# The inversion of 16-wide diagonal blocks, moved from VectorE to GpSimd

## The chip, the cores and the metric

The kernel runs on one core of one Trainium2 chip. The metric is the device time of one execution in microseconds (us). A core has five engines that run side by side: TensorE (PE in the profile; its weight loads are PEld), VectorE (DVE), ScalarE (ACT), GpSimd (POOL) and SyncE (SP), which here only issues DMAs. Each works through its own queue in order and waits on semaphores for the others.

## The reference

Two layers of a backbone on 128 context tokens and 1024 latent tokens, width 1024. Layer 0 is attention, layer 1 is recurrent: a retention part and an RWKV-7 part, each with 8 heads of 64, each in both directions. A feed-forward block follows each layer. The part that the change touches is the RWKV-7 scan:

```python
def rwkv7_scan(r, w, k, v, a_vec, b_vec, s0):
    def step(S, inp):
        rt, wt, kt, vt, at, bt = inp
        sa = jnp.einsum('bhvk,bhk->bhv', S, at)
        S = S * wt[:, :, None, :] + sa[..., None] * bt[:, :, None, :] + vt[..., None] * kt[:, :, None, :]
        return S, jnp.einsum('bhvk,bhk->bhv', S, rt)
    ...
    S, ys = lax.scan(step, s0, xs)
    return jnp.moveaxis(ys, 0, 1), S
```

## The kernel before

The kernel runs in stages: attention layer with its projections, feed-forward block, projections of the recurrent layer, the recurrence (`rec_scan`), its output projection, feed-forward block. The recurrence lies between about 2420 and 3000 us of the span.

`rec_scan` does not step token by token. The nine chunks of 128 tokens are taken for four heads at a time (two pairs of heads, both directions), which makes 18 units `m`. Within a unit the coupling of the tokens of a chunk is a triangular 128x128 matrix per head and direction, and its inverse is wanted. The loop over `m` builds unit `m` while it finishes earlier ones:

- `prep(m)` loads the unit's columns (F, V), and makes AR, BK, PC and HT on VectorE, ScalarE and GpSimd (lines 1149 to 1175).
- `amat(m, i)`, for i = 0 and 1, multiplies AR and BK on TensorE (line 1190) into two PSUM banks; VectorE writes the masked parts to TC, ARB and KK (lines 1192, 1193, 1194: one **mask group** for each of eight products). TC holds the triangular matrices.
- `inv16(m)` inverts the 16-wide diagonal blocks. ScalarE copies them out of TC (C, line 1225); they go to memory and come back with one block on each of 32 partitions (bts, BT: lines 1226, 1230); VectorE mirrors them for the other half (line 1231), which gives 64 partitions. MB starts as the unit matrix (line 1233, GpSimd). Then 15 steps, each of a product (line 1240, tf) and a sum (line 1241, MB), invert all blocks. Each instruction needs the one before it. Step j works on 15-j rows of j+1 columns, so an instruction has 15 to 64 elements on each of 64 partitions. VectorE **folds** the two halves (lines 1243 and 1244, into BT); the result goes out to memory and comes back spread over 128 partitions (mbs, ML: lines 1247, 1249), and is multiplied with a block mask into E (VectorE) and MM (GpSimd), line 1254.
- `values(m)` makes two products with KK (lines 1206, 1213).
- `levels(m-1)` widens the inverses of the unit before from 16 to 32, 64 and 128: for each level a masked copy (E, line 1270, GpSimd), transposes (1264), a masked product (WT, line 1272, VectorE), two matrix products (1275, 1280) with a ScalarE copy between (X, 1277), and merges on VectorE (1282, 1284). At the end VectorE writes Nf and Nb (line 1290).
- `chain(m-2)` carries the state through the unit (lines 1306 to 1340; Zs on GpSimd in line 1328).

BT, MB, C, ML and TC are few: one buffer each of BT, MB, C and ML, three of TC. In the first units, pieces of an output projection (lines 81 to 83, with VectorE's line 769) are woven in as filler. The order in which each engine's queue holds all this is fixed when the kernel is built: a scheduler runs through the program with a cost for every instruction, so a change of engine can reorder the queues of all engines in this stage.

Of the kernel before, what the change touches and what calls it, by code (L numbers as in the profile page):

```python
# [15 lines left out]
ALU = mybir.AluOpType  # L16
# [20 lines left out]
def dap(ap, offset, dims):  # L37
    return bass.AP(tensor=ap.tensor, offset=ap.offset + offset, ap=dims)
# [5 lines left out]
class Net:  # L44
# [1015 lines left out]
    def rec_scan(self, hp):  # L1060
        nc, I, O = self.nc, self.I, self.O
        hp.release()
        with ExitStack() as es:
# [155 lines left out]
            def inv16(m):  # L1219

                tc, bd, md = TC[m % NTC], bts[m % 2], mbs[m % 2]
                C = self.t(p1, [P, 4, 32], tag="C")
                for g in range(4):
                    gs = slice(32 * g, 32 * g + 32)
                    nc.scalar.copy(C[gs], tc[gs, :, gs])
                nc.sync.dma_start(bd.rearrange("u p i -> p u i"), C)
                bt = self.t(p1, [64, 256], tag="BT")
                for b in range(2):
                    src = dap(bd, b * 16 * 33, [[32 * 32, 16], [32, 16], [1, 16]])
                    nc.sync.dma_start(bt[16 * b : 16 * b + 16].rearrange("p (j i) -> p j i", i=16), src)  # L1230
                nc.vector.tensor_copy(bt[32:64], bt[0:32, ::-1])
                mb = self.t(p1, [64, 256], tag="MB")
                nc.gpsimd.tensor_copy(mb, eye)
                B3 = bt.rearrange("p (j i) -> p j i", i=16)
                M3 = mb.rearrange("p (i c) -> p i c", c=16)
                for j in range(15):
                    nr, ncl = 15 - j, j + 1
                    tt = self.t(p1, [64, 64], tag="tf")[:, : nr * ncl].rearrange("p (i c) -> p i c", c=ncl)
                    row, col = B3[:, j, j + 1 :].unsqueeze(2).to_broadcast([64, nr, ncl]), M3[:, j : j + 1, :ncl].to_broadcast([64, nr, ncl])
                    nc.vector.tensor_tensor(tt, row, col, op=ALU.mult)  # L1240
                    nc.vector.tensor_tensor(M3[:, j + 1 :, :ncl], M3[:, j + 1 :, :ncl], tt, op=ALU.add)  # L1241
                m2 = bt[0:32]
                nc.vector.tensor_copy(m2, mb[32:64, ::-1])
                nc.vector.tensor_tensor(m2, m2, mb[0:32], op=ALU.add)
                for b in range(2):
                    dst = dap(md, b * 256, [[512, 16], [16, 16], [1, 16]])
                    nc.sync.dma_start(dst, m2[16 * b : 16 * b + 16].rearrange("p (i c) -> p i c", c=16))
                ml = self.t(p1, [P, 4, 16], tag="ML")
                nc.sync.dma_start(ml, md.rearrange("u p c -> p u c"))
                sh = [P, 4, 8, 16]  # L1250
                bm = lambda i: blk[:, i, :].rearrange("p (b c) -> p b c", c=16).unsqueeze(1).to_broadcast(sh)
                MM, E = self.t(p, [P, 4, P], tag="MM"), self.t(p, [P, 4, P], tag="E")
                for t, i, eng in ((E, 1, nc.vector), (MM, 0, nc.gpsimd)):
                    eng.tensor_tensor(t.rearrange("p u (b c) -> p u b c", c=16), ml.unsqueeze(2).to_broadcast(sh), bm(i), op=ALU.mult)
                Q["MM", m] = MM, E
# [126 lines left out]
            for m in range(NH + 2):  # L1382
# [10 lines left out]
                for ops in ORDER:  # L1393
                    for o in ops:
                        if o == "c":
                            step(cha)
                        elif o == "l":
                            step(lev)
                        elif o == "f":
                            pull()  # L1400
                        elif o == "p" and m < NH:
                            prep(m)
                        elif m < NH and o == "a":
                            amat(m, 0)
                        elif m < NH and o == "b":
                            amat(m, 1)
                            if m == 0:
                                nc.scalar.dma_start(eye, I["k_eye"])
                                for t, n in ((blk, "k_blk"), (mE, "k_mE"), (mO, "k_mO"), (tri, "k_tri")):
                                    nc.scalar.dma_start(t, I[n].rearrange("l p c -> p l c"))  # L1410
                        elif m < NH and o == "i":
                            inv16(m)
                        elif m < NH and o == "v":
                            values(m)
# [637 lines left out]
```

## Time and profile before

| | |
|---|---|
| three runs | 3990.24, 3992.53, 3998.9 us (median 3992.53) |
| profiled execution, its own time | 3991.86 us |
| span of the profiled execution | 3990.1 us |
| busy over the span | PE 95%, PEld 89%, DVE 54%, ACT 31%, POOL 18% |
| mean granted clock of TensorE | 0.973 of full speed |

Busy is the time in which an engine executed an instruction. The profiled execution has marks for start and end of each instruction, and who released a wait is inferred from semaphores. Matmuls are pipelined and their ends are modelled, so TensorE's busy time is no exact measure of work. The instruction counts of the page are 5159 on DVE and 730 on POOL.

### The profile page before, as it was taken

To read this page: it belongs to the slowest core of one execution; us is meant where nothing else is said; L and a number is where in the kernel's file an instruction comes from. 1 tells how busy PE (TensorE), PEld (TensorE's weight loads), DVE (VectorE), ACT (ScalarE), POOL (GpSimd) and SP (SyncE) were. 2 spreads that over 40 slices of the span, in tenths; PEclk is the share of its full clock that TensorE was granted. 3 is DMA by queue.
4 is the path that set the end of the run, shared out by engine and by line. 5 is a ranking of instruction groups with operands and counts; after the bars stand their busy time and mean duration, and the time that the engine had idled before them with its cause. 6 is when DMAs were issued, how large, how long until landed. Compare 5 with 4: busy or idle time off the path is not lost.

```text
span 3990.1 us, 62872 instructions
## 1 busy us (share of the span) xinstructions
PE 3790.7 (95%) x23989; PEld 3559.6 (89%) x23989; DVE 2169.5 (54%) x5159; ACT 1250.4 (31%) x2930; POOL 711.9 (18%) x730
## 2 busy tenths in 40 slices
PE   8999997999999999998999998888888999999998
PEld 5899997999999999998989876776777999999998
DVE  5666665666454545345254656888875543343343
ACT  4555545555111111115232322233222411111112
POOL 3321202202100000012011232233322300000000
PEclk9999998999999999999999997999999999999999
DMA  6533316432222222213243434222223211111111
GB/s 203 150 105 91 95 52 163 126 85 88 67 80 64 85 64 80 69 46 116 87 129 102 163 123 142 66 70 63 64 64 103 64 38 45 41 37 43 43 40 53
DMA packets 378086, 339.98 MB, mean 85 GB/s; under 512 B 65428, under 2 KB 328720, under 8 KB 376248
## 3 DMA queue, kind: packets, MB, share of 16 engines
q1 hardware_dynamic: 359344, 324.37, 27.0%
q10 hardware_dynamic: 13160, 7.27, 0.7%
q0 software_dynamic: 5280, 4.31, 0.5%
q8 instruction: 190, 3.11, 0.3%
q14 instruction: 112, 0.92, 0.1%
HBM read 263.37 MB, written 72.38 MB: 84 GB/s over the span
## 4 chain that ended last, share of the span: by engine, by line
PE 78%; DVE 10%; DMA 5%; issue 3%; ACT 2%; POOL 1%; SPq 0%; ACTq 0%; DVEq 0%; POOLq 0%
PE mm L81 17%; PE mm L83 17%; PE mm L82 17%; PE o L522 3%; PE mm L390 2%; PE mm L392 2%; PE mm L391 2%; PE T L516 1%; DVE MB L1241 1%; DVE tf L1240 1%; PE mm L857 1%; PE A L1190 1%; PE mm L859 1%; PE mm L858 1%; PE S L558 1%
## 5 line engine op out<-in xcount | busy, mean ns | idle before, releaser
L81 PE MATMUL mm<-hH,wh 128*128 128x384 f32 x2544 | 865.1, 341 | 20.2 <-DVE nv L363 12.6
L82 PE MATMUL mm<-hL,wh 128*128 128x384 f32 x2544 | 860.6, 339 | 2.5 <-DVE hL L366 2.5
L83 PE MATMUL mm<-hH,wl 128*128 128x384 f32 x2544 | 859.8, 339 | 0.0
L769 DVE SCALAR_TENSOR_TENSOR x<-mm,mod,x 128x384 f32<-128x384 f32 (+2 forms) x896 | 431.5, 512 | 197.5 <-PE mm L83 195.8
L81 PEld LDWEIGHTS mm<-hH,wh 128*128 128x128 f32 x2544 | 480.0, 189 | 31.4 <-ACT wh L73 18.8
L82 PEld LDWEIGHTS mm<-hL,wh 128*128 128x128 f32 x2544 | 480.1, 189 | 5.6 <-DVE hL L366 2.7
L83 PEld LDWEIGHTS mm<-hH,wl 128*128 128x128 f32 x2544 | 480.0, 189 | 4.0 <-issue 2.9
L1692 POOL TENSOR_TENSOR gl<-fs,gh 128x384 fp32r<-128x384 f32 x132 | 140.4, 1063 | 1484.1 <-ACT gh L1691 1484.1
L74 DVE TENSOR_TENSOR wl<-wraw,wh 128x512 fp32r<-128x512 f32 (+2 forms) x360 | 217.9, 618 | 336.0 <-ACT wh L73 306.4
L82 PE MATMUL mm<-gl,owh 128*128 128x384 f32 x1056 | 353.0, 334 | 0.0
L83 PE MATMUL mm<-gh,owl 128*128 128x384 f32 x1056 | 352.9, 334 | 0.0
L81 PE MATMUL mm<-gh,owh 128*128 128x384 f32 x1056 | 350.4, 335 | 0.0
L1690 DVE TENSOR_TENSOR fs<-fs,mm 128x384 f32<-128x384 f32 x132 | 73.0, 553 | 430.3 <-PE mm L83 424.7
L73 ACT CAST wh<-wraw 128x512 fp32r<-128x512 f32 (+2 forms) x360 | 188.2, 530 | 205.5 <-DMA wraw<-in_w_ffn_in_dram 77.3
L73 ACT CAST owh<-owraw 128x1024 fp32r<-128x1024 f32 x60 | 62.9, 1049 | 489.7 <-PE mm L82 446.0
L390 PE MATMUL mm<-wh,hH 128*128 128x384 f32 x576 | 199.3, 346 | 3.8 <-ACT ist L408 3.7
L82 PEld LDWEIGHTS mm<-gl,owh 128*128 128x128 f32 x1056 | 198.3, 188 | 0.1
L83 PEld LDWEIGHTS mm<-gh,owl 128*128 128x128 f32 x1056 | 198.2, 188 | 0.0
L81 PEld LDWEIGHTS mm<-gh,owh 128*128 128x128 f32 x1056 | 197.8, 188 | 0.3 <-DVE x L769 0.3
L391 PE MATMUL mm<-wl,hH 128*128 128x384 f32 x576 | 195.3, 339 | 0.0
L392 PE MATMUL mm<-wh,hL 128*128 128x384 f32 x576 | 194.0, 338 | 0.0
L1689 ACT ACTIVATE fs<-mm 128x384 f32<-128x384 f32 x132 | 64.9, 492 | 383.5 <-PE mm L83 383.4
(385 smaller groups left out, 7437.8 us busy)
## 6 DMA issues: line engine op xcount, KB each, us to landing
wraw<-in_w_ffn_in_dram SPq DMA_DIRECT2D x352, 128.0 KB
aw<-in_w_ada_dram SPq DMA_DIRECT2D x160, 256.0 KB
owraw<-in_w_ffn_out_dram SPq DMA_DIRECT2D x44, 512.0 KB
F<-stg SPq DMA_DIRECT2D x34, 640.0 KB
stg<-st SPq DMA_DIRECT2D x12, 1536.0 KB
qkv<-ist SPq DMA_DIRECT2D x72, 192.0 KB
wraw<-in_w_in_attn_dram SPq DMA_DIRECT2D x64, 192.0 KB
nab<-rpbd SPq DMA_DIRECT2D x64, 192.0 KB
```

The lines of the kernel that those rows point to most:

```text
L73: nc.scalar.copy(hi, src)
L74: nc.vector.tensor_tensor(lo, src, hi, op=ALU.subtract)
L81: mm(out, lhsT=wh, rhs=xh, start=first, stop=False)
L82: mm(out, lhsT=wh, rhs=xl, start=False, stop=False)
L83: mm(out, lhsT=wl, rhs=xh, start=False, stop=last)
L390: mm(pt[:, :ncol], lhsT=hH[k][:, c], rhs=WH[k], start=k == 0, stop=False)
L391: mm(pt[:, :ncol], lhsT=hH[k][:, c], rhs=WL[k], start=False, stop=False)
L392: mm(pt[:, :ncol], lhsT=hL[k][:, c], rhs=WH[k], start=False, stop=k == KT - 1)
L522: nc.tensor.matmul(o, lhsT=pT[:, i * P : (i + 1) * P], rhs=vs(b + i), start=b + i == 0, stop=b + i == nk - 1)
L769: self.nc.vector.scalar_tensor_tensor(x[f][:, c], pt[:, a:b], self.mod[l][jg][:, f, cd : cd + 1], x[f][:, c], op0=ALU.mult, op1=ALU.add)
L1690: nc.vector.tensor_tensor(s, s, pg[1][:, :GW], op=ALU.mult)
L1692: nc.gpsimd.tensor_tensor(gl[:, sl], s, gh[:, sl], op=ALU.subtract)
```

## The change

The product and the sum of the 15 steps are issued on GpSimd instead of VectorE. Nothing else in the program text changes; operands, sizes and buffers are the same.

```diff
                 for j in range(15):
                     nr, ncl = 15 - j, j + 1
                     tt = self.t(p1, [64, 64], tag="tf")[:, : nr * ncl].rearrange("p (i c) -> p i c", c=ncl)
                     row, col = B3[:, j, j + 1 :].unsqueeze(2).to_broadcast([64, nr, ncl]), M3[:, j : j + 1, :ncl].to_broadcast([64, nr, ncl])
-                    nc.vector.tensor_tensor(tt, row, col, op=ALU.mult)
-                    nc.vector.tensor_tensor(M3[:, j + 1 :, :ncl], M3[:, j + 1 :, :ncl], tt, op=ALU.add)
+                    nc.gpsimd.tensor_tensor(tt, row, col, op=ALU.mult)
+                    nc.gpsimd.tensor_tensor(M3[:, j + 1 :, :ncl], M3[:, j + 1 :, :ncl], tt, op=ALU.add)
```

The queues change with it. VectorE, around the fold of one unit (BT_28734, MB_28738) in the steady part of the stage; TC_4880 belongs to the next unit. Before:

```order
L1241 TENSOR_TENSOR MB_28738<-MB_28738,tf_28782 64x15 [waits DVE_49]
L1284 COPY_PREDICATED MM_28464<-mO_24512,I_28809 128x512 [waits PE_49]
L1243 COPY BT_28734<-MB_28738 32x256 [waits DVE_49]
L1192 COPY_PREDICATED TC_4880_24532<-msk_4873_24523,A_29036 128x128 [waits PE_49]
L1193 COPY_PREDICATED ARB_4885_24537<-msk_4873_24523,A_29036 128x128
L1244 TENSOR_TENSOR BT_28734<-BT_28734,MB_28738 32x256 [waits DVE_49]
L1194 COPY_PREDICATED KK_4878_24528<-msk_4873_24523,A_29036 128x256
L1192 COPY_PREDICATED TC_4880_24532<-msk_4873_24523,A_29037 128x128 [waits PE_49]
```

In the changed kernel:

```order
L1284 COPY_PREDICATED MM_28464<-mO_24512,I_28676 128x512
L1243 COPY BT_28734<-MB_28738 32x256 [waits Pool_49]
L1192 COPY_PREDICATED TC_4880_24532<-msk_4872_24522,A_29024 128x128 [waits PE_49]
L1193 COPY_PREDICATED ARB_4884_24536<-msk_4872_24522,A_29024 128x128
L1194 COPY_PREDICATED KK_4877_24527<-msk_4872_24522,A_29024 128x256
L1244 TENSOR_TENSOR BT_28734<-BT_28734,MB_28738 32x256 [waits DVE_49]
L1192 COPY_PREDICATED TC_4880_24532<-msk_4872_24522,A_29025 128x128 [waits PE_49]
L1193 COPY_PREDICATED ARB_4884_24536<-msk_4872_24522,A_29025 128x128
L1194 COPY_PREDICATED KK_4877_24527<-msk_4872_24522,A_29025 128x256
L1272 TENSOR_TENSOR WT_28795<-I_28796,mE_24511 128x512 [waits PE_49]
L1192 COPY_PREDICATED TC_4880_24532<-msk_4873_24523,A_29036 128x128 [waits DVE_49,PE_49]
```

The fold's copy waits for GpSimd; the last four mask groups of the next unit (A_29024, A_29025, A_29036, A_29037) and a WT stand behind it, where before only two groups did.

GpSimd, from the unit matrix MB of that unit on. Before:

```order
L1233 COPY MB_28738<-eye_24521 64x256 [waits DVE_49]
L1167 TENSOR_TENSOR BK_5983_28910<-F_5978_28897,EN_28902 128x512 [waits DMAHW0_49,PE_49,Activation_49]
L1254 TENSOR_TENSOR MM_28464<-ML_28462,blk_24524 128x512 [waits DMAHW4_49]
L1270 TENSOR_TENSOR E_28602<-MM_28464,mE_24511 128x512 [waits Pool_49]
L1328 TENSOR_TENSOR Zs_28700<-SB_4888_24540,PC_27897 128x512 [waits PE_49]
L1165 TENSOR_TENSOR AR_5973_28880<-F_5969_28872,EL_28876 128x2x128 [waits PE_49]
L1270 TENSOR_TENSOR E_28660<-MM_28464,mE_24511 128x512 [waits DVE_49]
L1164 COPY PC_28871<-EL_28901 128x2 [waits Activation_49]
L1165 TENSOR_TENSOR AR_5982_28905<-F_5978_28897,EL_28901 128x2x128 [waits PE_49]
```

In the changed kernel:

```order
L1233 COPY MB_28738<-eye_24521 64x256 [waits DVE_49,Pool_49]
L1254 TENSOR_TENSOR MM_28464<-ML_28462,blk_24524 128x512 [waits DMAHW3_49]
L1270 TENSOR_TENSOR E_28602<-MM_28464,mE_24511 128x512 [waits PE_49,Pool_49]
L1240 TENSOR_TENSOR tf_28740<-BT_28734,MB_28738 64x15 [waits DMAHW6_49,DMAHW5_49,DVE_49]
L1241 TENSOR_TENSOR MB_28738<-MB_28738,tf_28740 64x15 [waits Pool_49]
L1167 TENSOR_TENSOR BK_5983_28910<-F_5978_28897,EN_28902 128x512 [waits DMAHW0_49,PE_49,Activation_49]
L1240 TENSOR_TENSOR tf_28743<-BT_28734,MB_28738 64x28 [waits Pool_49]
L1328 TENSOR_TENSOR Zs_28700<-SB_4888_24540,PC_27897 128x512 [waits PE_49]
L1241 TENSOR_TENSOR MB_28738<-MB_28738,tf_28743 64x14x2 [waits Pool_49]
L1240 TENSOR_TENSOR tf_28746<-BT_28734,MB_28738 64x39 [waits Pool_49]
```

The 30 instructions stand between the first E and the next unit's BK, with one BK, Zs, two AR, two PC and one E among them, and each waits for GpSimd itself. The two AR follow the sixth and the seventh pair. MM of the unit before goes ahead of the first.

SP, the transfers at the end of that unit's inversion. Before:

```order
L1247 DMA mbs_24563<-BT_28734 16x256 [waits DMAHW6_49]
L1226 DMA bts_24562<-C_29048 128x4x32 [waits DMAHW7_49,Activation_49]
L1249 DMA ML_28789<-mbs_24563 128x4x16 [waits DMAHW6_49,DMAHW5_49,DMAHW0_49]
L1230 DMA BT_29054<-bts_24562 16x16x16 [waits DMAHW7_49,DMAHW1_49]
L1230 DMA BT_29054<-bts_24562 16x16x16 [waits DMAHW2_49]
```

In the changed kernel:

```order
L1247 DMA mbs_24563<-BT_28734 16x256 [waits DMAHW6_49]
L1249 DMA ML_28789<-mbs_24563 128x4x16 [waits DMAHW7_49,DMAHW6_49,DMAHW5_49]
L1226 DMA bts_24562<-C_29048 128x4x32 [waits DMAHW0_49,Activation_49]
L1230 DMA BT_29054<-bts_24562 16x16x16 [waits DMAHW1_49,DMAHW0_49,Pool_49]
L1230 DMA BT_29054<-bts_24562 16x16x16 [waits DMAHW2_49]
```

The load of ML goes ahead of the store of the next unit's blocks.

## Rows read from the trace of the kernel before

**Rows 1.** The page, part 1: busy us, share of the span and instructions of each engine

```profile
PE 3790.7 (95%) x23989; PEld 3559.6 (89%) x23989; DVE 2169.5 (54%) x5159; ACT 1250.4 (31%) x2930; POOL 711.9 (18%) x730
```

**Rows 2.** Chain of waits of the recurrence stage: shares by line; start us, us, what

```profile
by line: DVE MB L1241 7.3%; DVE tf L1240 7.3%; issue 6.5%; PE A L1190 5.5%; DVE MM L1284 4.4%; DVE KK L1194 4.3%; PE I L1275 3.5%; PE I L1280 3.1%; PE mm L81 2.8%; DVE ARB L1193 2.7%; DVE TC L1192 2.7%; PE I L1264 2.7%; DVE WT L1272 2.6%; P
...
2553.88 1.20 DVE tf L1240
...
2823.68 1.14 DVE tf L1240
...
2853.02 1.14 DVE tf L1240
...
2942.74 1.14 DVE tf L1240
```

**Rows 3.** Windows: stretch, length, busy PE, PEld, DVE, ACT, POOL, clock, DMA share, GB/s

```profile
2500.00:2530.00 30.00, 29.66 (x250) 26.15 (x249) 28.06 (x81) 9.75 (x20) 7.45 (x7) 1.00 0.22 60
2820.90:2850.30 29.40, 25.88 (x219) 20.98 (x218) 25.45 (x74) 9.29 (x23) 10.20 (x12) 1.00 0.26 69
```

**Rows 4.** VectorE in order of time, one turn: start us, us, instruction, [idle before]

```profile
2839.59 0.29 DVE L1192 COPY_PREDICATED TC<-msk,A 128x128 f32<-128x128 int32 x1
...
2840.32 0.28 DVE L1192 COPY_PREDICATED TC<-msk,A 128x128 f32<-128x128 int32 x1
...
2841.15 0.67 DVE L1272 TENSOR_TENSOR WT<-I,mE 128x512 f32<-128x512 f32 x1
...
2843.12 0.72 DVE L1240 TENSOR_TENSOR tf<-BT,MB 64x15 f32<-64x15 f32 x1
...
2845.31 0.28 DVE L1243 COPY BT<-MB 32x256 f32<-32x256 f32 x1
...
2846.03 0.41 DVE L1244 TENSOR_TENSOR BT<-BT,MB 32x256 f32<-32x256 f32 x1
...
2846.69 0.28 DVE L1192 COPY_PREDICATED TC<-msk,A 128x128 f32<-128x128 int32 x1
...
2850.79 0.86 DVE L1254 TENSOR_TENSOR E<-ML,blk 128x512 f32<-128x512 f32 x1 [2.10 <-DMA ML<-mbs]
```

**Rows 5.** Line 1240, whole span: duration ns min/median/max

```profile
L1240 DVE TENSOR_TENSOR tf<-BT,MB x270: 158/201/1265, 2435.6 to 2956.9; 64x15 f32<-64x15 f32 x18, 64x39 f32<-64x39 f32 x18, 64x55 f32<-64x55 f32 x18, 64x63 f32<-64x63 f32 x18
```

**Rows 6.** GpSimd in order of time, two pieces of the stage

```profile
2669.86 1.76 POOL L1254 TENSOR_TENSOR MM<-ML,blk 128x512 f32<-128x512 f32 x1 [0.64 <-DMA ML<-mbs]
2671.70 1.27 POOL L1270 TENSOR_TENSOR E<-MM,mE 128x512 f32<-128x512 f32 x1
...
2833.18 0.19 POOL L1164 COPY PC<-EL 128x2 f32<-128x2 f32 x1
...
2842.52 1.29 POOL L1167 TENSOR_TENSOR BK<-F,EN 128x512 f32<-128x512 f32 x1 [5.52 <-ACT X L1277]
```

**Rows 7.** GpSimd by line, whole span: count, busy us, mean ns, idle before

```profile
L1270 POOL TENSOR_TENSOR E<-MM,mE 128x512 f32<-128x512 f32 x36 | 47.9, 1332 | 50.6 <-DVE MM L1284 27.8 <-DVE MB L1241 9.2 <-DVE tf L1240 6.5
L1167 POOL TENSOR_TENSOR BK<-F,EN 128x512 f32<-128x512 f32 x36 | 46.5, 1292 | 127.1 <-ACT BH L1170 50.3 <-ACT X L1277 37.8 <-issue 21.7
...
L1165 POOL TENSOR_TENSOR AR<-F,EL 128x256 f32<-128x256 f32 x36 | 26.8, 745 | 32.7 <-PE c L1336 32.7
...
L1328 POOL TENSOR_TENSOR Zs<-SB,PC 128x512 f32<-128x512 f32 x14 | 14.7, 1051 | 0.9 <-PE c L1314 0.9
...
L1164 POOL COPY PC<-EL 128x2 f32<-128x2 f32 x36 | 9.6, 268 | 87.7 <-ACT EL L1157 87.6
```

**Rows 8.** Lines 1254 and 437, whole span: duration ns min/median/max, forms

```profile
L1254 DVE TENSOR_TENSOR E<-ML,blk x18: 691/693/1773, 2459.2 to 2963.2; 128x512 f32<-128x512 f32 x18
L1254 POOL TENSOR_TENSOR MM<-ML,blk x18: 1269/1764/1772, 2459.2 to 2963.2; 128x512 f32<-128x512 f32 x18
...
L437 POOL TENSOR_TENSOR rm<-rm,rm x40: 451/461/1486, 99.9 to 575.1; 128x128 f32<-128x128 f32 x32, 128x512 f32<-128x512 f32 x8
```

## The prediction

> **What bounds the kernel now.** I read the page first, then the chain of waits over the recurrence stage, then that stage in windows, and last one turn of it on each engine. On the whole span the change looks harmless: GpSimd is busy 18% and VectorE 54% [rows 1], and TensorE carries the kernel. But an average over stages says nothing about the one stage that is edited. The inversion runs only there, from 2435 to 2960 us. In the chain of waits of that stage its two lines are the first two entries, 7.3% each, ahead of every TensorE line [rows 2]. Its first instruction recurs at a steady beat: from 2553.88 to 2942.74 us lie 13 turns, 29.9 us each, and the turn that I take apart begins at 2823.68 and ends at 2853.02, so it lasts 29.34 us [rows 2].
>
> In that turn VectorE is busy 25.45 of 29.40 us, TensorE 25.88, GpSimd 10.20 [rows 3]. TensorE's ends are modelled, so its number is a ceiling; VectorE's is work in one queue, in order. That queue makes the turn: the inversion starts at 2823.68, its last result is folded at 2845.31, the last diagonal mask of the next unit's scores is written at 2846.69 (0.28 us), and 6.05 us after its end, at 2853.02, the next inversion starts [rows 2, 4]. In those 6.05 us the diagonal blocks are copied, go out to memory and come back. So the turn is one loop: inversion, masks behind it in the queue, a trip through memory, the next inversion. Whatever holds the inversion longer or shorter moves the turn by as much.
>
> **What goes from VectorE.** 30 instructions a turn, 540 in all. Undisturbed one takes 0.20 us (median), but up to 1.27 us [rows 5]: where GpSimd runs a two-input instruction, VectorE's small product waits for its end, as the one at 2843.12, which took 0.72 us beside a GpSimd product of 1.29 us that began at 2842.52 [rows 4, 6]. VectorE gets back 6.0 us a turn at the median, more with these waits. That is not the gain, for the loop does not vanish: VectorE's fold (line 1243) now waits for GpSimd's last step, and the last four mask groups of the next unit stand behind that fold. The moved queue still closes the loop; only its parts get other lengths.
>
> **The new turn, part by part.**
>
> (a) From GpSimd's last step to the last mask on VectorE: the fold's copy 0.28, a mask group 0.73 (2839.59 to 2840.32), the fold's sum 0.41, a group 0.73, the transposed factor's product 0.67, a group 0.73, the last mask 0.28 [rows 4]. Together 3.83 us. The first two groups' score products do not depend on GpSimd, and each later product needs only a bank that an earlier group has freed.
>
> (b) From that mask to the next start, 6.05 us as now [rows 2, 4]: the same copies and the same two transfers. On SP's queue the load of the folded inverses (ML) now goes ahead of the blocks' store instead of behind it; it is issued early enough that neither waits for the other. On GpSimd MM (1.76 us) and the first E (1.27 us) now stand between two inversions [rows 6]. They need ML, which lands about 4.4 us after the fold's sum (2846.03 plus 0.41, to 2850.79, where VectorE's product on ML starts after a wait of 2.10 us [rows 4]), so they are through about 9 us after the last step (0.28 + 0.73 + 0.41 + 4.4 + 1.76 + 1.27 = 8.9), ahead of the 9.9 us of (a) and (b): covered, by 1 us.
>
> (c) The 30 steps on GpSimd. No row has so small a two-input instruction on GpSimd. The nearest: 128x128 at 0.46 us median [rows 8] and 128x512 at 1.27 us [rows 6]. That is 2.1 ns an element and 0.19 us fixed, and a copy of 2 elements at 0.19 us undisturbed [rows 6] fits that fixed part. The 15 products touch 680 elements a partition, the 15 sums as many, 1360 in all: 30 x 0.19 + 1360 x 0.0021 = 8.6 us. Each step needs the one before it; E, which needs MM, starts 0.08 us after its end (2669.86 + 1.76 to 2671.70) [rows 6]. 30 x 0.08 = 2.4 us. Together 11.0 us, or 0.37 us a step. Broadcast operands cost nothing extra that shows: MM has two and reaches 1.27 us undisturbed [rows 8].
>
> (d) The other GpSimd work now woven between the steps: one BK 1.29, one Zs 1.05, two AR 0.75 each, two PC 0.27 each, one E 1.33 [rows 7], 5.7 us. These means hold the collisions with VectorE's two-input instructions.
>
> The new turn: 3.83 + 6.05 + 11.0 + 5.7 = 26.6 us, against 29.34: 2.8 us less. Over 13 turns, 36 us. **The other terms:** the first four turns (2435 to 2554 us) also carry an output projection and TensorE is busy 29.66 of 30 us in their midst [rows 3], so I count nothing there; if that cover of TensorE work is thinner than it looks, the same 2.8 us a turn would add some 10 us of gain. The last inversion has no next turn; nothing. The new wait on VectorE (line 1243) has masks, E, Nf and Nb behind it, and ScalarE's block copy and TensorE's value products wait for those masks; that is (a) and (b). Who else waits on GpSimd: AR, which feeds the next unit's score products, now stands behind six and seven pairs of steps. By my count it is ready about 9 us after the inversion starts, and the two levels of products, masks and merges that follow it on TensorE and VectorE end some 2 us before GpSimd's last step (an estimate from the durations of this turn). That is the next thing to be late.
>
> The profiled execution took 3991.86 us (median of the runs 3992.53, so 0.7 us below it). 3991.86 - 36 = **3956 us**.
>
> **A rule that speaks against it.** On the same line and shape (1254, 128x512) VectorE took 0.69 us and GpSimd 1.27 us undisturbed, 1.84 times [rows 8]. The Trainium skill, "GPSIMD Engine Reference", section "Engine selection", says to keep elementwise products and sums off GpSimd, which is about twice as slow on two inputs. Two times VectorE's 0.20 us make a step 0.40 us, the 30 with their gaps 14.4 us, the turn 30.0 us and the kernel some 8 us slower (an estimate by that page); the trace's large shape agrees with the page, and no row shows whether the factor holds where the fixed part rules.
>
> **Rivals.**
>
> *The factor holds for small steps too.* 0.20 x 1.84 = 0.37 us, with gaps 0.45 us a step, 13.4 us; the turn is 29.0 us, 0.3 us less: 4 us, about 3988 us, no change. For it: the ratio in [rows 8]. Against it: the fixed part of a GpSimd copy is 0.19 us, no more than a whole VectorE step. Chance 0.11.
>
> *GpSimd has a floor and the loop lengthens.* If a small two-input step costs as much as the smallest that the trace has, 0.46 us, it is 0.54 us with its gap: 16.2 us, turn 31.8 us, 2.4 us longer, 13 times 32 us: 4024 us. It decides from 0.46 us a step with gap (13.8 us for the 30), where the turn is back at 29.34. For it: no smaller product is in the trace, AR's collisions and TensorE's idling may add to the loop, and a wait on GpSimd stands in VectorE's queue with everything behind it. Against: 128, 256 and 512 elements (0.46, 0.75, 1.27 us) lie on one line with the copy's fixed part [rows 6 to 8]. Chance 0.19.
>
> *TensorE becomes the bound.* If its 25.88 us a turn are real work, the turn stops at 25.9 us: 3.4 x 13 = 45 us, 3947 us. It would show if the steps on GpSimd were cheaper than my sum. Chance 0.10.
>
> That the change does not do what it says is excluded: all 540 instructions stand on GpSimd in the order of the changed kernel.
>
> **How the numbers follow.** My forecast has 0.60. A step can be cheaper than I take it: without the gap the 30 steps are 8.6 us and the turn 24.2 us, 67 us less, 3925 us. That and TensorE's bound are the lower end. The dearer ends are the two first rivals; the range reaches up over "no change", to 3997 us, and leaves out the lengthened loop (0.19). A change of 0.2% is about 8 us, which is what a measurement of this kernel can tell from none. Faster: 0.60 + 0.10 = 0.70; within: 0.11; slower: 0.19.
>
> **What would show it.** In the changed profile lines 1240 and 1241 on GpSimd with a mean near 0.29 us and starts about 0.37 us apart; turns of 26 to 27 us; VectorE's busy time at 19 us a turn or less (25.45 [rows 3] less 30 x 0.20), GpSimd's near 19 (10.20 and 8.6); the chain of this stage on GpSimd's two lines, then on the fold, masks and the two transfers. I am wrong if a step is spaced 0.46 us or more, if GpSimd waits for AR's or E's inputs in the midst of the steps, or if MM rather than the blocks' load starts the next inversion.

## The result, and the profile after

The changed kernel took 3947.65 us (median of four runs, 3943.83 to 3961.69), the kernel before beside it 3991.39 us: a ratio of 0.9893, 95% interval 0.9866 to 0.992. It is 1.1% faster; 3956 us was forecast. The profiled execution took 3943.83 us, its span is 3942.0 us, 48.1 us shorter than the span before.

The page, part 1 (busy us, share of the span, instructions), answers to [rows 1]; beneath it the shares by line of the chain of waits of the stage, as in [rows 2]:

```profile
PE 3785.3 (96%) x23989; PEld 3557.3 (90%) x23989; DVE 2057.6 (52%) x4619; ACT 1246.1 (32%) x2930; POOL 852.0 (22%) x1270
```

```profile
by line: DMA F<-stg 7.1%; PE A L1190 6.1%; issue 5.8%; POOL tf L1240 5.3%; POOL MB L1241 5.1%; PE I L1280 4.6%; PE c L1314 4.5%; PE A L1206 4.0%; PE I L1275 3.6%; PE I L1264 3.5%; PE mm L81 3.4%; PE A L1213 3.4%; PE mm L82 3.2%; PE mm L83 3
```

The 540 instructions stand on GpSimd. The steps have gone from the head of the chain to its fourth and fifth place; ahead of them are now the transfer of F and TensorE's score products (line 1190), which the prediction did not have there. The two lines by themselves (duration ns min/median/max), which answer to [rows 5]:

```profile
L1240 POOL TENSOR_TENSOR tf<-BT,MB x270: 207/260/1196, 2426.6 to 2913.7; 64x15 f32<-64x15 f32 x18, 64x39 f32<-64x39 f32 x18, 64x55 f32<-64x55 f32 x18, 64x63 f32<-64x63 f32 x18
```

```profile
L1241 POOL TENSOR_TENSOR MB<-MB,tf x270: 211/278/516, 2427.9 to 2913.9; 64x15 f32<-64x15 f32 x18, 64x39 f32<-64x39 f32 x18, 64x55 f32<-64x55 f32 x18, 64x63 f32<-64x63 f32 x18
```

A product costs 0.26 us on GpSimd where it cost 0.20 us on VectorE: 1.3 times. Those are medians. On the mean, which holds the waits beside the other engine, the order is reversed, 276 ns for 297 (count | busy us, mean ns | idle before, of the kernel before and of the change):

```profile
L1240 DVE TENSOR_TENSOR tf<-BT,MB 64x15 f32<-64x15 f32 (+2 forms) x270 | 80.2, 297 | 5.8
L1240 POOL TENSOR_TENSOR tf<-BT,MB 64x15 f32<-64x15 f32 (+2 forms) x270 | 74.5, 276 | 51.0 <-DVE BT L1231 35.6
```

So the 30 instructions themselves hardly shorten the inversion: on the mean of thirteen steady turns their durations add up to 9.1 us before and 8.2 us now. What shortens it is the company that they keep: VectorE had some 33 other instructions between the first and the last of them, GpSimd has 7 (durations of 14.9 and 5.5 us in all). One inversion of each kernel as a window (stretch, length, busy PE, PEld, DVE, ACT, POOL, clock, DMA share, GB/s), in which VectorE ran 63 instructions before and GpSimd runs 38 now:

```profile
2823.68:2845.31 21.63, 18.82 (x155) 14.83 (x155) 20.68 (x63) 4.15 (x10) 6.64 (x8) 1.00 0.29 87
2794.57:2810.83 16.26, 15.92 (x145) 12.98 (x145) 10.88 (x24) 5.20 (x13) 13.28 (x38) 1.00 0.39 115
```

Now the end of one inversion on GpSimd, in order of time (start us, us, instruction, [idle before]), and the start of the next:

```profile
2810.33 0.21 POOL L1240 TENSOR_TENSOR tf<-BT,MB 64x15 f32<-64x15 f32 x1
2810.62 0.21 POOL L1241 TENSOR_TENSOR MB<-MB,tf 64x15 f32<-64x15 f32 x1
2810.80 1.26 POOL L1167 TENSOR_TENSOR BK<-F,EN 128x512 f32<-128x512 f32 x1
...
2821.51 0.21 POOL L1240 TENSOR_TENSOR tf<-BT,MB 64x15 f32<-64x15 f32 x1 [1.06 <-DVE BT L1231]
```

And VectorE beside it, which answers to [rows 4]:

```profile
2810.87 1.34 DVE L1243 COPY BT<-MB 32x256 f32<-32x256 f32 x1 [0.32 <-POOL MB L1241]
2812.23 0.30 DVE L1192 COPY_PREDICATED TC<-msk,A 128x128 f32<-128x128 int32 x1
...
2812.97 0.41 DVE L1244 TENSOR_TENSOR BT<-BT,MB 32x256 f32<-32x256 f32 x1
...
2815.40 0.30 DVE L1192 COPY_PREDICATED TC<-msk,A 128x128 f32<-128x128 int32 x1
```

The fold's copy (line 1243), 0.28 us before, takes 1.34 us: GpSimd's BK runs from 2810.80 to 2812.06, and the copy ends only behind it. All masks that stand behind the copy come 1.06 us later, and with them TensorE. By turns (windows: stretch, length, busy PE, PEld, DVE, ACT, POOL, clock, DMA share, GB/s), answering to [rows 3]:

```profile
2617.32:2647.43 30.11, 27.97 (x213) 23.12 (x212) 18.55 (x45) 8.51 (x22) 18.41 (x42) 0.89 0.25 68
2647.43:2679.79 32.36, 29.57 (x213) 24.29 (x212) 19.37 (x45) 8.70 (x22) 17.78 (x41) 0.84 0.22 62
...
2794.20:2821.15 26.95, 25.54 (x217) 20.96 (x216) 19.22 (x44) 9.11 (x23) 17.94 (x41) 1.00 0.28 76
```

Of the thirteen steady turns ten last 25.5 to 29.0 us, 27.15 on the mean, nearly all at full clock as the third row. Three last 30.1 to 32.4 us at a mean clock of 0.84 to 0.89 (the first two rows are two of them). What TensorE did ahead of that, in the turn of the first row (in order of time, then two windows):

```profile
2636.31 2.15 PE L1190 MATMUL A<-AR,BK 64*128 64x256 f32 x8 [1.46 <-DVE KK L1194]
...
2639.80 3.51 PE L1206 MATMUL A<-V,KK 128*128 128x64 f32 x16
```

```profile
2639.00:2643.00 4.00, 4.00 (x21) 4.00 (x20) 1.75 (x3) 1.01 (x4) 1.91 (x2) 0.50 0.21 30
...
2647.00:2651.00 4.00, 4.00 (x41) 3.80 (x43) 1.37 (x3) 2.73 (x7) 3.05 (x7) 1.00 0.00 0
```

TensorE sits idle for 1.46 us until VectorE's masks, which stand behind the delayed copy, have freed a bank; in the first window its granted clock is 0.50, the lower of its two levels (1.2 of 2.4 GHz), in the second it is back. In the turn that begins at 2794.20 the same wait lasts 1.07 us, the same 16 products take 1.90 us instead of 3.51, and the clock stays at 1.00.

Over the span the 48.1 us split as follows (starts of line 1231 and the last end of line 1290): the thirteen steady turns 389.0 to 365.1, 23.8 us; the first four 118.7 to 111.4, 7.4 us; the last inversion and what follows it in the stage 6.3 us; behind the stage 0.5 us; ahead of the first inversion 10.1 us. Whether the last of these is the change's is open: that start lies between 2414.4 and 2435.1 us in the fourteen profiles of this study, which is no steady figure, but the two kernels with the steps on VectorE have the two latest starts (2434.6 and 2435.1 us), and the twelve others lie at 2432.1 us or before.

### The profile page after: what moved, and what is told of

It is laid out like the page before. It is cut to its first block, busy times and chain, and to the rows that moved or that the text cites. A ratio compares the mean times of both kernels' runs of the same rounds, so it can differ in the third digit from the quotient of the medians.

```text
span 3942.0 us, 62994 instructions
## 1 busy us (share of the span) xinstructions
PE 3785.3 (96%) x23989; PEld 3557.3 (90%) x23989; DVE 2057.6 (52%) x4619; ACT 1246.1 (32%) x2930; POOL 852.0 (22%) x1270
## 4 chain that ended last, share of the span: by engine, by line
PE 81%; DMA 5%; DVE 4%; POOL 3%; issue 2%; ACT 2%; SPq 0%; ACTq 0%; DVEq 0%; POOLq 0%
PE mm L81 17%; PE mm L82 17%; PE mm L83 17%; PE o L522 3%; PE mm L390 2%; PE mm L392 2%; PE mm L391 2%; PE mm L857 1%; PE T L516 1%; DMA F<-stg 1%; PE mm L858 1%; PE mm L859 1%; PE A L1190 1%; DMA aw<-in_w_ada_dram 1%; POOL tf L1240 1%
## 5 line engine op out<-in xcount | busy, mean ns | idle before, releaser
L81 PEld LDWEIGHTS mm<-hH,wh 128*128 128x128 f32 x2544 | 480.5, 189 | 30.1 <-ACT wh L73 18.8
```

The lines of the kernel that those rows point to most:

```text
L81: mm(out, lhsT=wh, rhs=xh, start=first, stop=False)
```

## The experiments

Each kernel's time is given by its ratio to the kernel before, run on the same chip; the change's own is 0.9893. The table has means over the thirteen steady turns of each profile, from lines 1231, 1240, 1241 and 1243 (us; in kernels with inserted lines these instructions have other numbers, 1245 and 1247 for the last two in e9); the clock is TensorE's mean granted clock from 2560 to 2860 us. "Fold" is the copy of line 1243; between the last step and it lie 0.0 to 0.1 us but for 0.4 in the kernel before, 0.7 in e6 and 4.8 in e10; what is left of the turn is the wait from line 1231 to the first step, 0.4 to 1.7 us.

| | ratio, 95% interval | turn | the 15 steps | fold | fold to next start | clock |
|---|---|---|---|---|---|---|
| before | 1 | 29.92 | 21.12 | 0.28 | 7.09 | 0.99 |
| the change | 0.9893 (0.9866 to 0.992) | 28.09 | 16.35 | 1.16 | 10.08 | 0.95 |
| e1 fold's copy on ScalarE | 0.9855 (0.9838 to 0.9872) | 26.58 | 16.29 | 0.41 | 9.49 | 0.99 |
| e2 half the steps | 0.9905 (0.9888 to 0.9923) | 29.71 | 7.84 | 0.84 | 20.58 | 0.93 |
| e3 half the steps, before | 0.9933 (0.9917 to 0.995) | 30.77 | 9.27 | 0.28 | 20.62 | 0.93 |
| e4 products twice | 0.9883 (0.9867 to 0.9899) | 27.98 | 19.29 | 0.28 | 6.58 | 0.97 |
| e5 one column | 0.99 (0.9883 to 0.9917) | 28.72 | 14.39 | 0.28 | 13.66 | 0.95 |
| e6 PC on ScalarE | 0.9872 (0.9847 to 0.9897) | 27.54 | 15.52 | 1.11 | 9.77 | 0.95 |
| e7 whole fold off VectorE | 0.9905 (0.9882 to 0.9928) | 29.32 | 17.96 | 0.40 | 10.56 | 0.90 |
| e8 e1 and e6 | 0.9812 (0.9796 to 0.9828) | 26.50 | 15.31 | 0.40 | 10.32 | 1.00 |
| e9 twice, masks behind | 1.0035 (1.0021 to 1.0048) | 32.04 | 20.19 | 1.17 | 9.85 | 0.83 |
| e10 half, masks ahead | 0.9819 (0.9803 to 0.9835) | 26.39 | 9.54 | 0.28 | 11.42 | 1.00 |
| e11 e7, E last | 0.9819 (0.9803 to 0.9835) | 25.95 | 16.43 | 0.40 | 8.72 | 0.99 |
| e12 e11 and e6 | 0.9799 (0.9784 to 0.9814) | 25.39 | 14.19 | 0.40 | 10.30 | 1.00 |

The scheduler lays out every kernel anew. VectorE's queue in one steady turn (m is a mask group of the next unit, c and s the fold's copy and sum, E the product that waits for ML; other work left out):

```
before   m m m m m m c m s m E
change   m m m m c m s m m m E
e2, e3   c s m m m E m m m m m
e4       m m m m m m m m c s E
e5       m m m c m s m m E m m
e10      m m m m c s m m m m E
```

**e1, the fold's copy on ScalarE**

```diff
-                nc.vector.tensor_copy(m2, mb[32:64, ::-1])
+                nc.scalar.copy(m2, mb[32:64, ::-1])
```

> The changed kernel with the fold's copy (line 1243) on ScalarE; nothing else. In the profile of the change that copy takes 1.34 us on VectorE, where 0.28 us was foreseen, beside a GpSimd instruction of 1.26 us that follows the last step; and in four of the thirteen steady turns TensorE idles before the masks' products and its clock is low behind that (turns of 29.0 to 32.4 us beside 26.7 to 27.4 us in the others). Theory A, the wait for the neighbour engine causes both: the fold's end comes 0.9 us sooner, TensorE's idle time ahead of line 1190 falls from 1.0 to 1.5 us to some 0.3 us, and there are fewer long turns: 12 us (0.9 x 13) to 35 us below the change. Theory B, the long turns come from TensorE's own chain of products, AR and the transfer of F, and the fold only shares the time: at most 5 us below the change, with as many long turns.

Measured: 3933.1 us, 0.38% below the change by the ratios, 15 us. The intervals just overlap; the traces decide: turns fall by 1.5 us, half of it in the fold's copy itself, TensorE's waits ahead of line 1190 are down to 0.43 us at most, and the clock of the stretch is 0.99. Theory A. (Of the four long turns that the expectation names, the one of 28.95 us ran at full clock.) GpSimd, ScalarE and VectorE at the end of one inversion:

```profile
2799.28 1.28 POOL L1167 TENSOR_TENSOR BK<-F,EN 128x512 f32<-128x512 f32 x1
```

```profile
2799.35 0.41 ACT L1243 COPY BT<-MB 32x256 f32<-32x256 f32 x1 [3.37 <-POOL MB L1241]
```

```profile
2799.53 0.44 DVE L1194 COPY_PREDICATED KK<-msk,A 128x256 f32<-128x256 int32 x1
2799.87 0.97 DVE L1244 TENSOR_TENSOR BT<-BT,MB 32x256 f32<-32x256 f32 x1
```

The same BK now delays neither ScalarE's copy nor VectorE's masks, only the two-input sum (0.97 us for 0.41).

**e2 and e3, half the steps, of the change and of the kernel before**

```diff
-                for j in range(15):
+                for j in range(0, 15, 2):
```

> The changed kernel with every second of the 15 steps left out (8 are left, so the inverses are not those of the reference): 14 GpSimd instructions and 672 of 1360 elements a partition fewer a turn, 5.1 us a turn by the spacing that the change's profile shows (0.35 us). Theory A, the loop through the inversion makes the turn, and TensorE's 25.6 us are the next limit: turns fall from 28.1 us on the mean to 25.7 us, about 30 us below the change (66 us if there were no limit). Theory B, only VectorE's relief brought the gain and GpSimd's steps lie beside other work: the time of the change, within 8 us. Theory C, TensorE binds the changed kernel already: within 8 us as well, with TensorE busy for all but a few tenths of a us of each turn in both.

> The kernel before with every second of the 15 steps left out (8 are left; the inverses are not those of the reference), all on VectorE: 14 instructions a turn fewer, 0.25 to 0.32 us each with their waits, 3.5 to 4.5 us a turn. Theory A, VectorE's queue with the inversion in it makes the turn of 29.9 us: 13 x 3.5 to 4.2 (TensorE's 25.7 us end it) = 45 to 55 us below the kernel before, with the first four turns a little more. Theory B, another limit (TensorE, or the transfers) holds the turn: less than 15 us below.

Measured: e2 is no faster than the change, and e3 gained 0.7% over the kernel before, all outside the steady turns (first four 118.7 to 100.5 us; the thirteen 389.0 to 400.0). No theory had this. The steps take 8.5 and 11.9 us less, but 20.6 us pass from fold to next start. VectorE in e2:

```profile
2765.62 0.43 DVE L1194 COPY_PREDICATED KK<-msk,A 128x256 f32<-128x256 int32 x1
2768.27 0.69 DVE L1254 TENSOR_TENSOR E<-ML,blk 128x512 f32<-128x512 f32 x1 [2.21 <-DMA ML<-mbs]
2768.88 0.29 DVE L1192 COPY_PREDICATED TC<-msk,A 128x128 f32<-128x128 int32 x1
...
2773.81 0.29 DVE L1192 COPY_PREDICATED TC<-msk,A 128x128 f32<-128x128 int32 x1
```

With an earlier fold the scheduler put it ahead of all eight mask groups, and E's wait for ML ahead of five of them: the trip of the folded blocks and that of the next blocks now follow one another. What these two kernels show is the price of a place in VectorE's queue; on the loop they decide nothing by themselves. e10 takes that up.

**e4, each product twice**

```diff
                     nc.gpsimd.tensor_tensor(tt, row, col, op=ALU.mult)
+                    t2 = self.t(p1, [64, 64], tag="tg")[:, : nr * ncl].rearrange("p (i c) -> p i c", c=ncl)
+                    nc.gpsimd.tensor_tensor(t2, row, col, op=ALU.mult)
```

> The changed kernel with each product of the 15 steps issued twice on GpSimd, the second into a tile that nobody reads: 15 instructions a turn more, 15 x 0.19 + 680 x 0.0021 = 4.3 us, of which up to 1 us lies in the gap before the sum. Theory A, the inversion on GpSimd is in the loop that makes the turn: 3.3 to 4.3 us a turn, 43 to 56 us above the change, about the time of the kernel before. Theory B, GpSimd's length lies beside other work and VectorE's relief is the gain: no more than 10 us above the change.

Measured: 3946.39 us, the time of the change, as theory B had it; but the table gives another reason than B's. The steps do take 2.9 us more, and the fold to the next start 3.5 us less, for all eight mask groups stand ahead of the fold; the fold's copy takes 0.9 us less, for GpSimd's BK now stands among the steps and not behind the last. e9 takes that up.

**e5, one column**

```diff
-                    nr, ncl = 15 - j, j + 1
+                    nr, ncl = 15 - j, 1
```

> The changed kernel with one column in each of the 15 products and sums (15 - j elements a partition, where it has 15 to 64), so all columns but the first are left out of the inverses. The 30 instructions stay, with 240 elements for 1360: by the change's own rows (0.21 us for 15 elements, 0.28 to 0.31 us for 55 to 64) some 2.4 us less a turn. The queues keep their order but for a few places, unlike with half the steps, where VectorE's masks were moved behind the wait for ML and 20.6 us instead of 10.1 us passed from the fold to the next start. Theory A, the inversion on GpSimd closes the loop of the turn: its span falls from 16.35 us to 14.0 us, the mean turn from 28.1 to about 25.7 us, 20 to 31 us below the change. Theory B, the steps wait in their queue for AR, PC and the transfer of F anyway: the span falls by less than 1 us, at most 10 us below the change.

Measured: 3952.54 us, within the noise of the change. The steps fell by 2.0 us, as A had it, but the copy and E moved up by a group or two, and fold to next start rose by 3.6 us. So neither theory holds as a whole. I had taken the few changed places for harmless; they were the ones that count.

**e6, PC on ScalarE**

```diff
-                    nc.gpsimd.tensor_copy(PC[:, :, d : d + 1], el[:, :, pc : pc + 1])
+                    nc.scalar.copy(PC[:, :, d : d + 1], el[:, :, pc : pc + 1])
```

> The changed kernel with the copy of two elements to PC (line 1164) on ScalarE, behind the exponential that it reads; VectorE's and SP's queues keep their order. On GpSimd that copy stands among the 15 steps, takes 0.19 to 0.45 us and waits 0.45 to 0.57 us for ScalarE's exponential, which waits for the transfer of F (4.3 us), which waits for AR's read, which waits for a product of TensorE (line 1336). Theory A, this wait lies on the loop: the inversion's span falls by 0.6 to 1.2 us, 8 to 15 us below the change. Theory B, the next GpSimd instruction that reads the exponential (AR) waits as long in its place: the span stays within 0.3 us and the time within 5 us of the change.

Measured: the steps' span falls by 0.83 us with VectorE's order kept, as A had it; the turn falls by 0.55, since the fold then waits 0.6 us more for VectorE's masks ahead of it. The time (0.9872 for 0.9893) does not tell it from the change.

**e7, the whole fold off VectorE**

```diff
-                nc.vector.tensor_copy(m2, mb[32:64, ::-1])
-                nc.vector.tensor_tensor(m2, m2, mb[0:32], op=ALU.add)
+                nc.scalar.copy(m2, mb[32:64, ::-1])
+                nc.gpsimd.tensor_tensor(m2, m2, mb[0:32], op=ALU.add)
```

> The changed kernel with the fold's copy (line 1243) on ScalarE and its sum (line 1244) on GpSimd, so that VectorE's queue holds nothing that waits for the inversion. Theory A, the wait in VectorE's queue ties the masks to the inversion's end: masks and the next blocks' trip now run ahead of it, the next start comes some 5.5 us behind the last step (fold 1.0, store of the folded blocks 1.5 to 2.1, load of the next blocks 1.8, mirror 0.3) instead of 10, and TensorE's 25.6 us or a little more make the turn: 0 to 15 us below the kernel with the fold's copy on ScalarE alone, 15 to 35 us below the change. Theory B, TensorE's own chain through AR and F sets the turn when the collision is gone: within 5 us of the kernel with the fold's copy on ScalarE.

Measured: 3957.79 us (3934.55 to 3963.95), not below the change and 0.5% above e1. Neither theory. VectorE's wait is gone from the fold, but one for ML stands between two pieces of the last mask group; VectorE, TensorE and a window of e7:

```profile
2818.33 0.69 DVE L1254 TENSOR_TENSOR E<-ML,blk 128x512 f32<-128x512 f32 x1 [1.76 <-DMA ML<-mbs]
```

```profile
2819.63 0.43 PE L1206 MATMUL A<-V,KK 128*128 128x64 f32 x2 [1.39 <-DVE KK L1194]
```

```profile
2823.00:2826.00 3.00, 3.00 (x15) 2.90 (x14) 0.93 (x3) 1.49 (x3) 1.64 (x3) 0.50 0.00 0
```

Again TensorE is idle, for 1.39 us, ahead of the fall to the lower clock.

**e8, fold's copy and PC on ScalarE** (the edits of e1 and e6)

> The changed kernel with the fold's copy (line 1243) and the copy to PC (line 1164) both on ScalarE. Theory A, both waits lie on the loop and TensorE's 25.6 us a turn are not reached yet (26.6 us with the first edit alone): 5 to 12 us below the kernel with the first edit alone. Theory B, TensorE binds once the fold's copy is off VectorE: within 4 us of it.

Measured: 3915.59 us, 0.43% (17 us) below e1. But the thirteen turns gave 1.1 us of that (345.6 to 344.5); the first four gave 12.0 (113.8 to 101.8), the start of the stage 6.7, while what follows the stage took 3.3 us more; this study can't tell what of that is the edit's. For the steady turns this is B.

**e9, products twice, masks behind the fold.** The kernel of e4, and for each of the next unit's last four groups (`k`, line 1192)

```diff
+                        if m and i == 1:
+                            self.tc.add_manual_dep(k.ins, FOLD[m - 1].ins.name, ...)
```

which holds them behind the fold's copy in the queue.

> The kernel with each product issued twice on GpSimd again (its inversion spans 19.3 us for 16.4 us), but with one more edge for the scheduler: the last four mask groups of the next unit stand behind the fold's copy in VectorE's queue, as in the change. In the first such kernel all eight stood ahead of it, 6.6 us passed from the fold to the next start for 10.1 us in the change, and the turn stayed at 28.0 us. Theory A, the place of the masks hid the longer inversion: the turn is 0.4 to 1.7 + 19.3 + 0.3 to 1.2 + 9.5 to 10 = 30 to 32 us, 25 to 50 us above the change. Theory B, GpSimd's length is off the path whatever the order: within 10 us of the change.

Measured: 3995.74 us beside 3984.62 us before, 1.4% (57 us) above the change and slower than the kernel before. Theory A: turn 32.04, fold to next start 9.85. VectorE:

```profile
2812.62 1.33 DVE L1247 COPY BT<-MB 32x256 f32<-32x256 f32 x1 [1.57 <-POOL MB L1245]
...
2817.86 0.30 DVE L1192 COPY_PREDICATED TC<-msk,A 128x128 f32<-128x128 int32 x1 [0.67 <-PE A L1190]
```

The same instructions as in e4, in another order, cost 1.5%. The order differs on more than VectorE's queue: GpSimd has BK right behind the last step again, and the fold's copy beside it takes 1.17 us for 0.28. The held masks do open waits on TensorE: 2.0 to 3.5 us ahead of line 1190 in eleven of the thirteen turns, against a single one of 1.93 us in e4. But the clock falls with them, to 0.83 in the stretch, and TensorE's busy time of a turn rises from 25.78 to 29.72 us on the mean, nearly as much as the turn. How much of the 4.06 us is the masks' place and how much the clock is not separated.

**e10, half the steps, masks ahead.** The kernel of e2 with two edges the other way (in the masks' loop of unit m, behind group four for the fold's copy and behind group eight for E of unit m-1):

```diff
+                for x in LATE.pop((m - 1, i), ()):
+                    self.tc.add_manual_dep(x.ins, k.ins.name, ...)
```

> The changed kernel with every second step left out again (8 of 15), but with two edges for the scheduler that keep VectorE's order of the change: the fold's copy behind the fourth mask group of the next unit, and the product that waits for ML (E, line 1254) behind the eighth. Without them seven of the eight groups stood behind that wait, and 20.6 us passed from the fold to the next start. Theory A, that place alone cost the gain: some 10 us from the fold to the next start, and the turn falls to TensorE's 25.6 us or a little above (25.7 to 26.6 us): 20 to 32 us below the change. Theory B, something else holds the turn when the inversion is short: within 10 us of the change.

Measured: 0.9819 where e2 had 0.9905, 0.74% (30 us) below the change. Theory A: the two edges alone recover what e2 lacked (five groups stood behind E's wait there, not the seven of the expectation); GpSimd's order moved along (BK and Zs stand among the steps again). The fold now waits 4.8 us for the fourth group: the steps are off the path, and the turn of 26.4 us is made by the rest. So e10 does not show what a shorter inversion is worth: e1, with all fifteen steps and without the collision at the fold, has nearly the same turn (26.58 us).

**e11 and e12, E last.** e7 with the edge for E alone; e12 has e6's edit besides.

> The kernel with the whole fold off VectorE, with one edge for the scheduler: E's product (line 1254), which waits 1.76 us for ML, stands behind the last mask group and not between its pieces. In the kernel without that edge TensorE sits idle for 1.39 us before line 1206 behind that wait, and its granted clock is 0.83 to 0.92 in turns of 29.5 to 31.2 us. Theory A, that idle time is what costs the clock: the clock is 1.00 in nearly all turns, turns are 25.7 to 26.6 us, 15 to 35 us below the change. Theory B, the clock falls for another reason, or TensorE waits elsewhere as long: within 10 us of the kernel without the edge (3958 us).

> The whole fold off VectorE (copy on ScalarE, sum on GpSimd), the copy to PC on ScalarE, and E's product behind the last mask group. Theory A, nothing but TensorE's 25.6 us holds the turn any more: turns of 25.6 to 26.2 us, at or up to 15 us below the best kernel so far (fold's copy and PC on ScalarE, 3915.6 us). Theory B, the edge moves another wait into VectorE's queue (level products that wait for TensorE now stand first in it): 5 to 25 us above it.

Measured: e11 0.9819 for e7's 0.9905, 0.86% (34 us), turns of 25.95 us at a clock of 0.99, as theory A had them; that TensorE's idle time is what costs the clock does not follow from it (last section). e12 is the fastest, 3904.64 us (3897.83 to 3907.22), 2% below the kernel before and 0.94% (37 us) below the change; against e8 and e11 the intervals touch. The time is theory A's, but not the turns, which go below its 25.6 us. The first steady turn lasts 36.2 us (in most of the others a turn of more than 32 us comes among the first four), the other twelve 24.5 us on the mean. One of them, in a window:

```profile
2787.17:2811.63 24.46, 24.42 (x219) 20.67 (x218) 18.14 (x42) 10.05 (x26) 18.32 (x40) 1.00 0.30 83
```

TensorE is busy for 24.42 of 24.46 us. Here it is the bound, at less than the 25.9 us that I had read as its ceiling.

## Why the prediction was right, step by step

**The loop** (inversion, masks behind it, the trip through memory) gave the turn to about half a us where the clock was nearly full (26.6 for 27.15), and the cleanest tests are the small ones, with the order of VectorE's masks kept: 0.83 us off the steps took 0.55 us off the turn (e6), 0.76 us off the fold's copy took 1.5 us off, with the clock's part (e1). e4 and e9 point the same way, 4.06 us a turn apart, but the clock and BK's place changed along with the masks'. What failed is "moves the turn by as much": e4's steps are 2.9 us longer and its turn is no longer, since the scheduler gave the masks another place, and in e10 the steps are off the path.

**(c) and (d), 11.0 and 5.7 us.** 16.35 us measured for the 16.7, in part by luck. The starts of neighbours are 0.28 to 0.39 us apart (0.37 foreseen), and 30 steps at these distances make 10.3 us, 0.7 less than (c). Waits in the midst of the steps, which the sum did not have, fill the place: 0.26, 0.41 and 0.45 us in the turn that begins at 2794.57. 0.19 us and 2.1 ns an element, read from far larger shapes, held within 0.04 us down to 15 elements. That also settles two rivals. The factor of 1.84 for small steps falls: 1.3 by the medians. The floor of 0.46 us falls: 0.21 us was seen. The Trainium skill's rule ("GPSIMD Engine Reference", "Engine selection": about twice as slow on two inputs) holds here for 512 elements [rows 8] and not for 15 to 64.

**(a), 3.83 us: the term that was mis-sized.** In the turn from 2794.57 to 2821.51 the last step ends at 2810.83 and the last mask at 2815.70: 4.87 us, 1.06 of it the copy's delay behind BK. I had seen such collisions in [rows 4, 6] and priced none here. **(b), 6.05 us:** 5.81 us in that turn. So it lasts 26.94 us, for 26.6.

**The clock was not in the sum.** The three turns at a lower clock sum to 93.6 us, the ten others to 271.5, 27.15 on the mean: 12 us are lost in the three. The mean turn before was 29.92 (the one that I took apart, 29.34, was a short one), so at 27.15 throughout the thirteen would have given the 36 us forecast; they gave 23.8. e1 shows the collision's part: without it the mean turn is 26.58 us and the clock 0.99.

**What made up for it.** The first four turns and the end of the stage, which I had put at nothing, gave 7.4 and 6.3 us. That the cover of TensorE's filler work was thinner than 29.66 busy us of 30 suggest (the 10 us named for that case) fits e3, whose shorter steps cut the first four turns by 18.2 us; that the last inversion is followed by levels that wait for it fits e3 as well, which cut that part by 10.0 us. Neither was isolated. So 37.5 us came out of this stage for the 36, from other places: that the sum comes out so near is luck. The difference of the medians is 43.7 us.

**The signs.** VectorE at 19.2 us a turn and GpSimd at 17.9 (19 each foreseen) were right, and BT's load, not MM, starts the next inversion. The chain was not: it runs on a second loop, which I had named only as the next thing to be late. In order of time:

```profile
2827.20 0.43 PE c L1336 x2
2827.70 0.72 POOL AR L1165
2828.43 0.36 POOL tf L1240
2828.79 4.48 DMA F<-stg
2833.38 0.43 ACT EL L1157
2834.36 0.31 POOL MB L1241
...
2837.95 1.34 DVE BT L1243
...
2840.30 2.15 PE A L1190 x8
```

A product of the chain frees AR; AR's read frees F; F's transfer, the exponential and PC, which stands among the steps on GpSimd, hold the later steps, the fold, the masks and TensorE. The waits in the midst of the steps that I had named as a sign of error did occur: GpSimd waits for PC's exponential for 0.32 to 1.81 us in twelve of the thirteen turns, so there this second loop is the later of the two by that much. e6 takes 0.83 us off the steps by removing PC's wait.

**TensorE's bound** of 25.9 us a turn was too high: e12 has turns of 24.5 us. The measured 3947.65 us is the number of that rival (3947 us), but not its way: the mean turn is 28.09 us, and in the turn of 26.95 us TensorE is busy for 25.54.

Open: what shortened the first four turns in e8, how much of the 10.1 us ahead of the stage is the change's, and how much of e9's loss is the clock's.

## What to carry to other kernels

A wait that moves with an instruction is paid by what stands behind it in the waiting engine's queue, so read that queue's order for the new kernel before costing the move: the same work cost 1.5% more with four mask groups on the other side of one copy, the fall of TensorE's clock that came with it included. Count what stands between the moved instructions on either engine, too: here that shortened the inversion, and not the price of an instruction. An experiment that shortens or lengthens a step under a scheduler changes that order as well; hold the order with explicit edges, or the run answers another question. And when work goes to GpSimd, look at what it runs beside VectorE's instructions on the path, and at TensorE's granted clock turn by turn.

## What was not expected of the hardware

A copy from SBUF to SBUF on VectorE, with one input, waits for the end of a GpSimd two-input instruction like the two-input ones do: 1.34 us for 0.28, while predicated copies from PSUM (0.30, 0.44 us) and ScalarE's copy (0.41 us) beside the same instruction took their usual time. The Trainium skill, "SBUF — State Buffer", "Terms", has VectorE and GpSimd share a port pair that one holds for a whole instruction; the copy's 1.34 us beside BK's 1.26 us agrees, and the predicated copies show that not every VectorE instruction needs that pair.

TensorE's clock fell from 2.4 to 1.2 GHz (granted 1.00, then 0.50) behind single waits of 1.30 to 1.46 us in three turns of the change and of 1.39 us in e7; the three turns cost 12 us, far more than their waits. It did not fall behind waits of 1.43 to 1.47 us in three other turns of the change, nor behind eleven waits of 1.55 to 2.46 us in the steady turns of the kernel before, where it fell only twice. One of the eleven, in a turn whose clock is 1.00 [rows 3]:

```profile
2835.94 1.13 PE L1280 MATMUL I<-X,WT 128*128 128x128 f32 x8 [1.60 <-DVE tf L1240]
```

So the length of the one wait does not decide it; what does is open. Nor is it shown that fewer such waits bring the clock back: in e11 they are fewer than in e7 and the clock is 0.99 for 0.90, but the kernel before has many and 0.99 as well.
